# The second product of two MLPs by seven block products instead of eight

## The chip, the cores and the metric

The kernel runs on one core of a Trainium2 chip (trn2). The metric is the device time of one execution in microseconds. A profiled execution also leaves a trace of every instruction. Engines are named as in the profile: PE is the matrix engine (PEld its weight loads), DVE the vector engine, ACT the scalar engine, POOL the GpSimd engine, SP the engine that issues most DMAs.

## The reference

One sequence of 512 tokens of width 1024 goes through two layers. Layer 0 mixes tokens with a state-space scan, layer 1 with stick-breaking attention; each mixer is followed by an MLP of width 4096. Every sub-layer is residual and ends in a layer norm. All data are float32.

```python
def squared_relu_mlp(h, w1, w2):
    return jnp.square(jax.nn.relu(h @ w1)) @ w2

def reference(x, ...):
    h = x                                    # (1, 512, 1024)
    for layer in range(2):                   # w1[layer]: (1024, 4096), w2[layer]: (4096, 1024)
        mix = mamba2_mixer(h, ...) if layer == 0 else stick_breaking_attention(h, ...)
        h = layer_norm(ALPHA * h + mix, ln_mix_g[layer], ln_mix_b[layer])
        h = layer_norm(ALPHA * h + squared_relu_mlp(h, w1[layer], w2[layer]),
                       ln_mlp_g[layer], ln_mlp_b[layer])
    return h
```

## The kernel before

**Number format.** Every float32 matrix is split into two parts, `hi` (the value rounded to the matrix engine's format, made by a copy) and `lo` (the value less `hi`, made by a subtraction). A product `a @ b` is then three matmuls into the same bank of PSUM: hi·hi, hi·lo and lo·hi (`mm3`, lines 162 to 164). One matmul has a stationary block of 128 x 128 and moves 512 columns, or 256 in some stages.

**The stream of weights.** All weights are cut into tiles of 128 x 1024 float32 (512 KB) and put into one list, `stream`, in the order of their use. `emit_w` handles one tile: the DMA from memory into a buffer `raw` (line 139, issued by SP), the copy to `hi` on ACT (line 145), and the subtraction that gives `lo` on DVE (line 147; in the first stage of the kernel some are on POOL). `load_w` hands out the next tile and has those after it emitted. During an MLP there are four buffers for `raw` and six pairs for `hi` and `lo` (four in the pool `wp`, two in the pool of the MLP), used in turn.

**The MLP** (`mlp`). The 4096 inner units are made in two halves of 16 blocks of 128 units. For each block, 24 matmuls (8 blocks of the depth by three) with the weights stationary and the 512 tokens moving give one bank `f1`. ACT takes it through ReLU and square (lines 356 and 357) into `r`, DVE makes the pair `hid` from it (lines 364 and 365). The first four blocks of a layer are made in `mlp_first`, by halves of the tokens. After 16 blocks `tok_out` forms the second product of this half: for each half `n` of the 1024 output columns, four banks for the four blocks of 128 tokens (`t`), with the activations stationary and 512 columns of weights moving; one weight tile holds two blocks of the depth and serves 24 matmuls. Each bank is added into the residual `v` by DVE (line 253 in the first half, which also scales by ALPHA; line 255 in the second).

**The end of an MLP.** In the second half and second column half, the last four weight tiles are taken group by group of tokens: by pairs of token blocks in layer 0 (`PAIRS`), by single blocks in layer 1. So a group is finished while the matmuls of the next group still run. For a finished group DVE takes statistics (line 257), `Norm.__call__` aggregates them (line 289), POOL makes the reciprocal root (lines 291 and 292), DVE shifts and scales the row (lines 295 and 299), and for layer 1 SP writes it out. In layer 0 `Norm.turn` transposes the row blocks on PE (line 330) and makes their pair on ACT and DVE (lines 333 and 334); the attention's first projections `pv`, `pq` and `pk` of the first 256 tokens can begin when the first pair of token blocks is turned.

**Order.** The program is written in one order; a planner in the compiler of the kernel language fixes from it, before the run, the order of instructions of each engine's queue, filling an engine's idle time with later work whose inputs and buffers it expects to be ready. Each engine then runs its queue in that fixed order and waits on semaphores.

Of the kernel before, what the change touches and what calls it, by code (L numbers as in the profile page):

```python
# [29 lines left out]
ALPHA = (2 * 2) ** 0.25  # L30
# [5 lines left out]
def trunk(ctx: ExitStack, tc: tile.TileContext, io):  # L36
    nc = tc.nc
# [3 lines left out]
    wp = ctx.enter_context(tc.tile_pool(name="wp", bufs=4))  # L41
# [42 lines left out]
    stream = []  # L84
    marks = []
    for g in range(G):
# [7 lines left out]
        if g % 4 == 3:  # L94
            stream += [io["w_so"][g // 4, n, i] for n in range(2) for i in range(4)]

    def mlp_stream(layer):
        for half in range(2):
            for m in range(16):
                stream.append(io["w1"][layer, half * 16 + m])  # L100
            for n in range(2):
                for i in range(8):
                    stream.append(io["w2"][layer, half, n, i])

    marks.append(len(stream))
    mlp_stream(0)
# [8 lines left out]
    stream += [io["w_o"][0, i] for i in range(4)] + [io["w1"][1, 0]]  # L115
    stream += [io["w_o"][1, i] for i in range(4)] + [io["w1"][1, 1]]
    marks.append(len(stream))
    mlp_stream(1)
    del stream[marks[2]:marks[2] + 2]
# [2 lines left out]
    taken = [0]  # L122
    extra = [None, 0, 0, True, 0]
    alt = {}

    def emit_w():
# [8 lines left out]
        if pool is not None and i % (2 + rb) >= 2:  # L135
            raw = pool.tile([P, 1024], F32, tag="rawx", name=f"wr{i}", bufs=rb)
# [8 lines left out]
        nc.scalar.copy(hi, raw)  # L145
        eng = nc.gpsimd if extra[3] and i % 4 == 1 else nc.vector
        eng.tensor_sub(lo, raw, f(hi))  # L147
# [12 lines left out]

    def mm3(out, a, b, start, stop, skip=False):
        nc.tensor.matmul(out, a[0], b[0], start=start, stop=False, skip_group_check=skip)  # L162
        nc.tensor.matmul(out, a[0], b[1], start=False, stop=False, skip_group_check=skip)  # L163
        return nc.tensor.matmul(out, a[1], b[0], start=False, stop=stop, skip_group_check=skip)  # L164

    def proj(out, w, r, c0=0, c1=T):
        for _ in proj_steps(out, w, r, c0, c1):
            pass
# [8 lines left out]
    class Filler:  # L177
# [4 lines left out]
        def add(self, gen):  # L182
            self.queue.append(gen)
# [152 lines left out]
    PAIRS = [(0, 1), (2, 3)]  # L336

    M0 = 4

    def mlp_first(layer, ln, ws):  # L340
        ws = ws + [load_w(io["w1"][layer, m]) for m in range(len(ws), M0)]
        pts = [psum("mm", [P, T], f"f1_{layer}0{m}") for m in range(M0)]
        for c in range(2):
            for m in range(M0):
                proj(pts[m], ws[m], ln.hl, c * 256, c * 256 + 256)
        return pts

    def mlp(layer, ln, nxt, pts):
        v, (hh, hl) = ln.v, ln.hl
        with tc.tile_pool(name=f"mlp{layer}", bufs=2, reuse_waits="tile") as mp:  # L350
            for half in range(2):
                hid = []

                def evac(m, pt):
                    r = mp.tile([P, T], F32, tag="r", name=f"r{layer}{half}{m}", bufs=2)
                    nc.scalar.activation(r, pt, AF.Relu)  # L356
                    nc.scalar.activation(r, r, AF.Square)  # L357
                    if m == 0:
                        hid.append(tuple(mp.tile([P, KD, T], F32R, tag="hid" + s, name=f"hd{layer}{half}0{s}", bufs=1)
                                         for s in "hl"))  # L360
                    elif m == 8:
                        hid.append(act_pair(f"hd{layer}{half}1"))
                    a, b = hid[m // 8]
                    nc.vector.tensor_copy(a[:, m % 8, :], r)
                    nc.vector.tensor_sub(b[:, m % 8, :], r, f(a[:, m % 8, :]))

                m0 = 0
                if half == 0:
                    m0 = M0
                    for m in range(M0):  # L370
                        evac(m, pts[m])
                    extra[:] = [mp, 2, 2, False, marks[1 + 2 * layer]]
                for m in range(m0, 16):
                    w = load_w(io["w1"][layer, half * 16 + m])
                    pt = psum("mm", [P, T], f"f1_{layer}{half}{m}")
                    proj(pt, w, (hh, hl))
                    evac(m, pt)

                def act(k, t):
                    a = hid[k // 8]  # L380
                    return tuple(x[:, k % 8, t * P:(t + 1) * P] for x in a)

                if half == 1:
                    nxt.load_rows(lambda j, c0: mp.tile([P, T if nxt.final else D], F32,
                                                        tag=f"lnr{j}{c0 if nxt.final else 0}",
                                                        name=f"lnr{layer}{j}{c0}", bufs=1),
                                  T if nxt.final else D)
                tok_out(f"f2_{layer}{half}", act, io["w2"][layer, half], v, half == 0, ("bg", "mm"),
                        None if half == 0 else ([(t,) for t in range(NT)] if nxt.final else PAIRS),
                        None if half == 0 else nxt)  # L390
        extra[:] = [None, 0, 0, False, 0]

    def ssm(sp, nxt_ln):
        x_h, x_l = act_pair("x_")
# [380 lines left out]
    def attention(ln, nxt):  # L775
        v, h_ = ln.v, ln.hl
# [3 lines left out]
        with tc.tile_pool(name="att", bufs=2, reuse_waits="tile") as at:  # L780
# [72 lines left out]
            def ao(*args):  # L853
                for _ in ao_steps(*args):
                    pass
# [17 lines left out]
            def ao_late(tt, turn):  # L873
                p0, p1 = ([psum(("mm", "bg")[n], [P, T], f"al{n}{t}") for t in tt] for n in range(2))
                if turn is None:
                    units_end = pin[0]
                    ao(p0, 0, tt, (6,), 6, 7)
                    w_1.append(load_w(io["w1"][1, 0]))
                    pin[0] = units_end
                with tc.issue_after(pin[0]):  # L880
                    if turn is None:
                        ao(p1, 1, tt, range(7), 0, 7)
                        ao(p0, 0, tt, (7,), 6, 7)
                    else:
                        ao(p0, 0, tt, (6, 7), 6, 7)
                    ao_evac(p0, 0, tt)
                    if turn is not None:
                        ao(p1, 1, tt, range(7), 0, 7)
                        w_1.append(load_w(io["w1"][1, 1]))
# [103 lines left out]
            w_o, wv_of, w_1, pin = {}, {}, [], [None]  # L993
# [4 lines left out]
            pts = [psum("mm", [P, T], f"p{'qk'[j]}0") for j in range(2)]  # L998
# [41 lines left out]
            pts = mlp_first(1, nxt, w_1)  # L1040
# [67 lines left out]
```

## Time and profile before

| | |
|---|---|
| median of 3 runs | 1461.16 us (1459.86 to 1462.78) |
| profiled execution, device time | 1463.09 us |
| its span, first to last instruction | 1460.7 us |
| PE busy | 1435.9 us (98%) |
| DVE busy | 864.2 us (59%) |
| ACT busy | 661.8 us (45%) |
| POOL busy | 219.9 us (15%) |
| mean granted PE clock | 0.996 |
| DMA | 129.43 MB, mean 89 GB/s |

Busy time is the union of an engine's instructions; matmuls overlap each other in the records, so a busy PE says only that no gap is seen. In a line of the groups, the figures after the bar are the busy time, the mean duration of one instruction in ns, and the engine's idle time just before them with what ended it. In a timeline, the columns are the start, the duration, and in brackets the idle time before the instruction and what released it. A table by windows gives the busy time of each engine in each stretch, the instructions in brackets, then the granted PE clock, the share of the DMA engines and GB/s.

### The profile page before, as it was taken

The page shows a single profiled execution, that of the slowest core. Times are in us where ns is not written, and L with a number is a line of the kernel's source. Part 1 is how long each engine was busy: PE and PEld are TensorE (multiplying, and loading weights), DVE is VectorE, ACT ScalarE, POOL GpSimd, SP SyncE. Part 2 cuts the span into 40 slices and gives each one's busy share as a digit, 9 for nine tenths or more (in the row PEclk, how much of TensorE's full clock was granted, in tenths as well). Part 3 has the DMA queues.
Part 4 walks back from the last instruction along what each step waited for, and adds up shares of the span by engine and source line. Part 5 has one row for each costly group of instructions (what it writes and reads, how often), then busy time and mean ns, then how long its engine had stood idle before and what let it go on. Part 6 is the DMA issues. An engine that isn't in the chain of part 4 may idle for free. (4 is left out here: it accounts for less than half of the span.)

```text
span 1460.7 us, 19159 instructions
## 1 busy us (share of the span) xinstructions
PE 1435.9 (98%) x7606; PEld 1235.5 (85%) x7606; DVE 864.2 (59%) x1274; ACT 661.8 (45%) x1072; POOL 219.9 (15%) x243
## 2 busy tenths in 40 slices
PE   8999999999999999999999999999999999999997
PEld 6898897888987988888888988898879888888886
DVE  5799897568877643234323667787866432244334
ACT  5566663346652442124322178888824332134210
POOL 2345554134442100000000100000000000000001
PEclk9999999999999999999999999999999999999999
DMA  5233222222123422332331121121224423322311
GB/s 180 73 101 103 71 73 73 87 87 71 60 73 127 161 91 98 101 94 94 101 100 61 57 87 58 44 73 59 73 64 137 132 87 101 102 92 95 101 44 58
DMA packets 37481, 129.43 MB, mean 89 GB/s; under 512 B 4496, under 2 KB 4752, under 8 KB 37392
## 3 DMA queue, kind: packets, MB, share of 16 engines
q1 hardware_dynamic: 34800, 123.88, 26.2%
q10 hardware_dynamic: 2592, 4.33, 1.0%
q8 instruction: 60, 0.98, 0.3%
q14 instruction: 29, 0.24, 0.1%
HBM read 126.10 MB, written 2.10 MB: 88 GB/s over the span
## 5 line engine op out<-in xcount | busy, mean ns | idle before, releaser
L147 DVE TENSOR_TENSOR wl<-wr,wh 128x1024 fp32r<-128x1024 f32 x202 | 249.3, 1235 | 432.0 <-ACT wh L145 431.4
L145 ACT CAST wh<-wr 128x1024 fp32r<-128x1024 f32 x219 | 230.3, 1053 | 542.9 <-PE f L164 252.6
L163 PE MATMUL f<-ln_hl,wh 128*128 128x512 f32 (+1 forms) x544 | 201.2, 371 | 0.0
L164 PE MATMUL f<-ln_hh,wl 128*128 128x512 f32 (+1 forms) x544 | 201.1, 370 | 0.0
L162 PE MATMUL f<-ln_hh,wh 128*128 128x512 f32 (+1 forms) x544 | 200.4, 371 | 0.0
L291 POOL TENSOR_SCALAR ln_rs<-ln_mv 128x2 f32<-128x2 f32 (+1 forms) x10 | 8.2, 816 | 739.5 <-DVE ln_mv L289 739.5
L164 PEld LDWEIGHTS f<-ln_hh,wl 128*128 128x128 f32 x544 | 102.3, 188 | 17.5
L163 PEld LDWEIGHTS f<-ln_hl,wh 128*128 128x128 f32 x544 | 102.3, 188 | 17.5
L162 PEld LDWEIGHTS f<-ln_hh,wh 128*128 128x128 f32 x544 | 101.9, 188 | 17.5
L164 PE MATMUL pz<-wh,x_l 128*128 128x256 f32 x256 | 72.7, 284 | 0.0
L163 PE MATMUL pz<-wl,x_h 128*128 128x256 f32 x256 | 72.5, 283 | 0.0
L162 PE MATMUL pz<-wh,x_h 128*128 128x256 f32 x256 | 72.3, 283 | 0.0
L147 POOL TENSOR_TENSOR wl<-wr,wh 128x1024 fp32r<-128x1024 f32 x17 | 43.6, 2562 | 93.4 <-ACT wh L145 93.0
L162 PE MATMUL px<-x_h,wh 128*128 128x512 f32 x128 | 50.8, 397 | 0.0
L163 PE MATMUL px<-x_l,wh 128*128 128x512 f32 x128 | 50.3, 393 | 0.0
L164 PE MATMUL px<-x_h,wl 128*128 128x512 f32 x128 | 50.2, 393 | 0.0
L163 PEld LDWEIGHTS pz<-wl,x_h 128*128 128x128 f32 x256 | 48.7, 190 | 0.9
L162 PEld LDWEIGHTS pz<-wh,x_h 128*128 128x128 f32 x256 | 48.7, 190 | 0.8
L164 PEld LDWEIGHTS pz<-wh,x_l 128*128 128x128 f32 x256 | 48.7, 190 | 0.4
L357 ACT ACTIVATE r<-r 128x512 f32<-128x512 f32 x64 | 40.4, 633 | 1.9
L356 ACT ACTIVATE r<-f 128x512 f32<-128x512 f32 x64 | 37.9, 591 | 6.0 <-PE f L164 5.9
L920 POOL TENSOR_TENSOR u<-u 128x128 f32<-128x128 f32 x16 | 7.8, 487 | 211.9 <-DVE u L918 211.9
(1369 smaller groups left out, 3842.0 us busy)
## 6 DMA issues: line engine op xcount, KB each, us to landing
wr<-w SPq DMA_DIRECT2D x128, 512.0 KB, 3.5
wr<-w_bc SPq DMA_DIRECT2D x16, 512.0 KB, 3.5
wr<-w_x SPq DMA_DIRECT2D x16, 512.0 KB, 3.5
wr<-w_z SPq DMA_DIRECT2D x16, 512.0 KB, 3.5
wr<-w_so SPq DMA_DIRECT2D x16, 512.0 KB, 3.5
wr<-w_qk SPq DMA_DIRECT2D x16, 512.0 KB, 3.5
wr<-w_v SPq DMA_DIRECT2D x8, 512.0 KB, 3.5
wr<-w_o SPq DMA_DIRECT2D x8, 512.0 KB, 3.4
```

The lines of the kernel that those rows point to most:

```text
L145: nc.scalar.copy(hi, raw)
L147: eng.tensor_sub(lo, raw, f(hi))
L162: nc.tensor.matmul(out, a[0], b[0], start=start, stop=False, skip_group_check=skip)
L163: nc.tensor.matmul(out, a[0], b[1], start=False, stop=False, skip_group_check=skip)
L164: return nc.tensor.matmul(out, a[1], b[0], start=False, stop=stop, skip_group_check=skip)
L291: nc.gpsimd.tensor_scalar(rs, self.mv[:, t0:t1, 1], LN_EPS, None, ALU.add)
L356: nc.scalar.activation(r, pt, AF.Relu)
L357: nc.scalar.activation(r, r, AF.Square)
L920: nc.gpsimd.tensor_add(e4[:, n:], e[:, P:2 * P], e[:, 2 * P:])
```

## The change

The inner units of each MLP are made in four quarters of 8 blocks of 128. In each quarter the second product is a matrix product of 512 tokens x 1024 units by 1024 units x 1024 columns, and it is cut into 2 x 2 blocks in tokens, units and columns and formed by seven block products (P1 to P7, Winograd's variant of Strassen's scheme) instead of eight. One block product uses two weight tiles; for each of them it has 12 matmuls (two token blocks by two depth blocks by three), so 24 in all. The matmuls have the same shape as before.

What is added or moved:

- The activations' four sums and the splits of seven operands (`prepare`, called twice in a quarter, after the fourth and the eighth block of units). The quarter's inner units stay in a tile `R`. Copies for `hi` are on ACT, sums and `lo` on DVE, each on 128 x 512 elements. The old copy to `hid` and its subtraction are gone.
- The weights' sums t1 to t4. They need the tiles of `w2` eight times per pass `s` instead of four (fetched again rather than kept), four extra subtractions of 128 x 1024 on DVE per pass, and seven split tiles instead of four. Two passes make a quarter.
- The buffers: two for `raw` instead of four, two each for t1 (`rawa`) and t2 (`rawc`); the six `hi`/`lo` pairs remain. `load_w` emits four tiles ahead instead of two in the MLP.
- The adds into `v`: 16 of 128 x 512 in a quarter. Bank pair X takes P1, is added to `v`, then P6 is accumulated onto it, it is added again, then P7, and it is added to two blocks of `v`. Bank pair Y takes P5, is added, then P3 is accumulated onto it and it is added.
- The end of an MLP: the last quarter's statistics and norm for the token blocks 0 and 1 follow P7, those for 2 and 3 follow P3 (by single blocks in layer 1). In layer 0 the turn of the blocks 0 and 1 is written between the two weight tiles of P3. The rows of the norm's gain and bias go to a tile of the pool `act`.
- The blocks of a quarter are made in the order 0, 4, 1, 5, 2, 6, 3, 7.

```diff
+    M_ORDER = (0, 4, 1, 5, 2, 6, 3, 7)
+    def w2_items(layer, q):
+        ...
+        for s in range(2):
+            key = (layer, q, s)
+            for nm, item in (("P1", b(0, 0, s)),
+                             ("P5", ("t1", key, b(0, 1, s), b(0, 0, s))),
+                             ("P6", ("t2", key, b(1, 1, s))),
+                             ("P4", ("t4", key, b(1, 0, s))),
+                             ("P7", ("t3", key, b(0, 0, s))),
+                             ("P2", b(1, 0, s)),
+                             ("P3", b(1, 1, s))):
...
     def mlp_stream(layer):
-        for half in range(2): ...
+        for q in range(4):
+            for m in range(8):
+                stream.append(w1_tile(layer, 8 * q + m))
+            for items in w2_items(layer, q).values():
+                stream.extend(items)
...
     def emit_w():
+        item = stream[i]
+        if not isinstance(item, tuple):
+            raw = fetch(item)
+        elif item[0] == "t1":
+            raw = sums[item[1]] = fetch(item[2], "rawa")
+            nc.vector.tensor_sub(raw, raw, fetch(item[3]))
+        elif item[0] == "t2":
+            raw = fetch(item[2], "rawc")
+            nc.vector.tensor_sub(raw, raw, sums[item[1]])
+            sums[item[1]] = raw
         else:
-            raw = wp.tile([P, 1024], F32, tag="raw", name=f"wr{i}", bufs=2)
-        nc.sync.dma_start(raw, stream[i])
+            raw = fetch(item[2])
+            if item[0] == "t3":
+                nc.vector.tensor_sub(raw, sums[item[1]], raw)
+            else:
+                nc.vector.tensor_sub(raw, raw, sums[item[1]])
...
-        prefetch(1 + 2)
+        prefetch(1 + depth[0])
...
+            extra[:] = [mp, 2, 0, False, marks[1 + 2 * layer]]
+            depth[0] = 4
+            def add(row, n, pts, stats=False, js=(0, 1)):
+                for j in js:
+                    t = rows[row][j]
+                    vs = v[:, t, n * T:(n + 1) * T]
+                    if (t, n) in started:
+                        nc.vector.tensor_add(vs, pts[j], vs)
+                    else: ...
+                    if stats:
+                        nc.vector.bn_stats(nxt.st[:, t, n, :], vs)
...
+                def prepare(c):
+                    ...
+                    def split(nm, src):
+                        h, l = (x[:, ks, :] for x in A[nm])
+                        nc.scalar.copy(h, src)
+                        nc.vector.tensor_sub(l, src, f(h))
+                    split("P1", a11)
+                    nc.vector.tensor_add(s1, a21, a22)
+                    nc.vector.tensor_sub(s2, s1, a11)
+                    nc.vector.tensor_sub(a21, a11, a21)
+                    split("P5", s1)
+                    split("P6", s2)
+                    split("P4", a22)
+                    split("P7", a21)
+                    split("P2", a12)
+                    nc.vector.tensor_sub(a12, a12, s2)
+                    split("P3", a12)
...
+                X = bank("bg", "X")
+                product("P1", X)
+                add(1, 0, X)
+                Y = bank("bg", "Y")
+                product("P5", Y)
+                add(2, 1, Y)
+                product("P6", X, False)
+                add(1, 1, X)
+                ...
+                Z = bank("mm", "Z")
+                product("P4", Z)
+                add(2, 0, Z)
+                product("P7", X, False)
+                add(2, 0, X, last)
+                add(2, 1, X, last)
+                if last:
+                    for g in ([(0,), (1,)] if nxt.final else [(0, 1)]):
+                        nxt(g)
+                Z = bank("mm", "V")
+                product("P2", Z)
+                add(1, 0, Z, last)
+                if not last:
+                    product("P3", Y, False)
+                    add(1, 1, Y)
+                elif nxt.final:
+                    ws = None
+                    for j in range(2):
+                        ws = product("P3", Y, False, (j,), None, ws)
+                        add(1, 1, Y, True, (j,))
+                        nxt((rows[1][j],))
+                else:
+                    product("P3", Y, False, mid=lambda: nxt.turn(rows[2]))
+                    add(1, 1, Y, True)
+                    nxt(rows[1])
+                    nxt.turn(rows[1])
```

More of the change, by code (lines that the diff above doesn't have):

```diff
@@ L95, in trunk, with w1_tile, b @@
             stream += [io["w_so"][g // 4, n, i] for n in range(2) for i in range(4)]
-    def mlp_stream(layer):
[L98 to L103, printed above, removed]
+    M_ORDER = (0, 4, 1, 5, 2, 6, 3, 7)
+    def w1_tile(layer, i):
+        return io["w1"][layer, 8 * (i // 8) + M_ORDER[i % 8]]
+    def w2_items(layer, q):
+        def b(row, n, s):
+            return io["w2"][layer, q // 2, n, 4 * (q % 2) + 2 * row + s]
+        r = {}
+        for s in range(2):
[7 more added lines that the diff above has]
+                             ("P3", b(1, 1, s))):
+                r.setdefault(nm, []).append(item)
+        return r
+    def mlp_stream(layer):
+        for q in range(4):
[3 more added lines that the diff above has]
+                stream.extend(items)
     marks.append(len(stream))
@@ L114, in trunk @@
     alt_o = len(stream) + 3
-    stream += [io["w_o"][0, i] for i in range(4)] + [io["w1"][1, 0]]
-    stream += [io["w_o"][1, i] for i in range(4)] + [io["w1"][1, 1]]
+    stream += [io["w_o"][0, i] for i in range(4)] + [w1_tile(1, 0)]
+    stream += [io["w_o"][1, i] for i in range(4)] + [w1_tile(1, 1)]
     marks.append(len(stream))
@@ L124, in trunk @@
     alt = {}
+    sums = {}
+    depth = [2]
     def emit_w():
@@ L340, in mlp_first @@
     def mlp_first(layer, ln, ws):
-        ws = ws + [load_w(io["w1"][layer, m]) for m in range(len(ws), M0)]
+        ws = ws + [load_w(w1_tile(layer, m)) for m in range(len(ws), M0)]
         pts = [psum("mm", [P, T], f"f1_{layer}0{m}") for m in range(M0)]
@@ L348, in mlp, with part @@
     def mlp(layer, ln, nxt, pts):
[L349 to L352, printed above, removed]
+        v, h_ = ln.v, ln.hl
+        W = P * 2
+        rows = {1: (2, 3), 2: (0, 1)}
+        cols = {1: slice(W, 2 * W), 2: slice(0, W)}
+        started = set()
+        with tc.tile_pool(name=f"mlp{layer}", bufs=1, reuse_waits="tile") as mp:
+            extra[:] = [mp, 2, 0, False, marks[1 + 2 * layer]]
[6 more added lines that the diff above has]
+                        nc.vector.tensor_add(vs, pts[j], vs)
+                    else:
+                        started.add((t, n))
+                        nc.vector.scalar_tensor_tensor(vs, vs, ALPHA, pts[j], ALU.mult, ALU.add)
+                    if stats:
+                        nc.vector.bn_stats(nxt.st[:, t, n, :], vs)
+            for q in range(4):
+                last = q == 3
+                R = act_tile(f"r{layer}{q}")
+                L = act_tile(f"l{layer}{q}", F32R).rearrange("p (a k) (b t) -> p a (k b) t", a=4, b=2)
+                def part(nm):
+                    return mp.tile([P, 4, W], F32R, tag=nm, name=f"{nm}{layer}{q}")
+                A = {nm: (part("h" + nm), L[:, i] if i < 4 else part("l" + nm))
+                     for i, nm in enumerate(("P1", "P5", "P6", "P7", "P2", "P3", "P4"))}
@@ L354, in evac @@
                 def evac(m, pt):
-                    r = mp.tile([P, T], F32, tag="r", name=f"r{layer}{half}{m}", bufs=2)
+                    r = R[:, m, :]
                     nc.scalar.activation(r, pt, AF.Relu)
                     nc.scalar.activation(r, r, AF.Square)
[L358 to L387, printed above, removed]
@@ L388, in mlp @@
-                tok_out(f"f2_{layer}{half}", act, io["w2"][layer, half], v, half == 0, ("bg", "mm"),
-                        None if half == 0 else ([(t,) for t in range(NT)] if nxt.final else PAIRS),
-                        None if half == 0 else nxt)
+                def prepare(c):
+                    ks, k2 = slice(2 * c, 2 * c + 2), slice(4 + 2 * c, 6 + 2 * c)
+                    a11, a21, a12, a22 = R[:, ks, cols[1]], R[:, ks, cols[2]], R[:, k2, cols[1]], R[:, k2, cols[2]]
+                    s1, s2 = (mp.tile([P, 2, W], F32, tag=nm, name=f"{nm}{layer}{q}{c}") for nm in ("u1", "u2"))
+                    def split(nm, src):
[13 more added lines that the diff above has]
+                    split("P3", a12)
@@ new lines, in mlp, with bank @@
+                for i in range(8):
+                    if q == 0 and i < M0:
+                        pt = pts[i]
+                    else:
+                        w = load_w(w1_tile(layer, 8 * q + i))
+                        pt = psum("mm", [P, T], f"f1_{layer}{q}{i}")
+                        proj(pt, w, h_)
+                    evac(M_ORDER[i], pt)
+                    if i % 4 == 3:
+                        prepare(i // 4)
+                items = w2_items(layer, q)
+                def bank(tag, nm):
+                    return [psum(tag, [P, T], f"{nm}{layer}{q}{j}") for j in range(2)]
@@ new lines, in product @@
+                def product(nm, pts, start=True, js=(0, 1), mid=None, ws=None):
+                    ah, al = A[nm]
+                    ws = {} if ws is None else ws
+                    for s in range(2):
+                        if s not in ws:
+                            ws[s] = load_w(items[nm][s])
+                        if s == 1 and mid is not None:
+                            mid()
+                        for kk in range(2):
+                            k, c = 2 * s + kk, slice(kk * T, (kk + 1) * T)
+                            for j in js:
+                                x = slice(j * P, (j + 1) * P)
+                                mm3(pts[j], (ah[:, k, x], al[:, k, x]), (ws[s][0][:, c], ws[s][1][:, c]),
+                                    start and k == 0, k == 3, skip=True)
+                    return ws
@@ new lines, in mlp @@
+                X = bank("bg", "X")
[7 more added lines that the diff above has]
+                if last:
+                    lnr = act_tile(f"lnr{layer}").rearrange("p k t -> p (k t)")
+                    wd = T if nxt.final else D
+                    nxt.load_rows(lambda j, c0: lnr[:, j * D + c0:j * D + c0 + wd], wd)
@@ L391, in mlp @@
         extra[:] = [None, 0, 0, False, 0]
+        depth[0] = 2
     def ssm(sp, nxt_ln):
@@ L877, in ao_late @@
                     ao(p0, 0, tt, (6,), 6, 7)
-                    w_1.append(load_w(io["w1"][1, 0]))
+                    w_1.append(load_w(w1_tile(1, 0)))
                     pin[0] = units_end
@@ L888, in ao_late @@
                         ao(p1, 1, tt, range(7), 0, 7)
[L889 removed]
+                        w_1.append(load_w(w1_tile(1, 1)))
                         nxt.turn(turn)
```

12 lines of the change are left out of this document (10 added, 2 removed).

## The prediction

> **What bounds the kernel now.** I read the page first, then the MLPs by windows, then single tiles, then timelines of the places where an MLP ends.
>
> ```profile
> span 1460.7 us, 19159 instructions
> PE 1435.9 (98%) x7606; PEld 1235.5 (85%) x7606; DVE 864.2 (59%) x1274; ACT 661.8 (45%) x1072; POOL 219.9 (15%) x243
> PEclk9999999999999999999999999999999999999999
> L147 DVE TENSOR_TENSOR wl<-wr,wh 128x1024 fp32r<-128x1024 f32 x202 | 249.3, 1235 | 432.0 <-ACT wh L145 431.4
> L145 ACT CAST wh<-wr 128x1024 fp32r<-128x1024 f32 x219 | 230.3, 1053 | 542.9 <-PE f L164 252.6
> ```
>
> A busy PE alone proves little, so the stretches of the two MLPs: second product (566 to 655), blocks of units (655 to 740), the end of layer 0 (800 to 830), the last second product and what follows it.
>
> ```profile
> core 0: us, PE busy (x) PEld busy (x) DVE busy (x) ACT busy (x) POOL busy (x), PEclk, DMA share, GB/s
> 566.00:655.00 89.00, 89.00 (x394) 73.68 (x394) 25.82 (x25) 19.00 (x19) 0.00 (x0) 1.00 0.29 95
> 655.00:740.00 85.00, 85.00 (x377) 70.38 (x376) 35.37 (x48) 32.75 (x46) 0.00 (x0) 1.00 0.31 99
> 800.00:830.00 30.00, 30.00 (x169) 26.19 (x168) 18.87 (x25) 5.06 (x7) 3.08 (x3) 1.00 0.13 38
> 1369.00:1452.00 83.00, 83.00 (x367) 68.41 (x365) 30.29 (x39) 10.55 (x10) 5.14 (x6) 1.00 0.17 56
> 1452.00:1461.00 9.00, 0.03 (x1) 0.00 (x0) 4.42 (x7) 0.00 (x0) 1.71 (x2) 0.67 0.30 110
> ```
>
> PE has no gap and the full clock until 1452, while DVE works 26 of 89 us in a second product. ACT and DVE wait for PE (the two groups above), not PE for them. So PE's pace sets the MLPs, and 9 us of norm and output stand behind its last matmul. The pace, from the inner units' tile (its users, first and last start):
>
> ```profile
> L356 ACT ACTIVATE r<-f x64: 577/592/601, 489.9 to 1365.8; 128x512 f32<-128x512 f32 x64
> L357 ACT ACTIVATE r<-r x64: 622/634/636, 490.5 to 1366.4; 128x512 f32<-128x512 f32 x64
> L364 DVE CAST hd001h<-r x8: 427/428/428, 524.5 to 562.6; 128x512 fp32r<-128x512 f32 x8
> L365 DVE TENSOR_TENSOR hd001l<-r,hd001h x8: 692/694/694, 525.0 to 563.1; 128x512 fp32r<-128x512 f32 x8
> L364 DVE CAST hd010h<-r x8: 427/428/428, 655.1 to 693.2; 128x512 fp32r<-128x512 f32 x8
> ```
>
> From block 8 of one half (524.5) to block 0 of the next (655.1) lie 8 x 24 + 384 = 576 matmuls in 130.6 us: 0.2267 us each; 562.6 - 524.5 over 7 x 24 gives the same. The Trainium skill ("TensorE: Matmul & The Clock Gate", the section that begins "Wait") has N / 2.4 GHz plus 2.5 ns, 0.2157 us at 512 columns; by that the first term below would be 41.4 us. The trace is slower, and its row decides.
>
> **The change, part by part.**
>
> *PE.* Before, 2 layers x 2 halves x 2 column halves x 16 depth blocks x 4 token blocks x 3 = 1536 matmuls in second products; after, 8 quarters x 7 products x 24 = 1344. 192 fewer x 0.2267 = **-43.5 us**, if PE stays fed. A product now takes 5.44 us, a weight tile 2.72 us instead of 5.44, a quarter 192 + 168 = 360 matmuls, 81.6 us.
>
> *DVE, total.* The slots, start to start:
>
> ```profile
> 501.61 1.23 DVE L147 TENSOR_TENSOR wl<-wr,wh 128x1024 fp32r<-128x1024 f32 x1 [1.01 <-ACT wh L145]
> 502.77 0.43 DVE L364 CAST hd000h<-r 128x512 fp32r<-128x512 f32 x1
> ...
> 1452.06 0.69 DVE L255 TENSOR_TENSOR v<-f,v 128x512 f32<-128x512 f32 x1 [0.45 <-PE f L164]
> 1452.79 0.69 DVE L257 BATCH_NORM_STATS2 ln_st<-v 128x6 f32<-128x512 f32 x1
> 1453.52 0.21 DVE L289 BATCH_NORM_AGGREGATE ln_mv<-ln_st 128x2 f32<-128x12 f32 x1
> 1453.76 1.42 DVE L295 SCALAR_TENSOR_TENSOR v<-v,ln_mv,lnr 128x512 f32<-128x512 f32 x2
> 1455.64 1.41 DVE L299 SCALAR_TENSOR_TENSOR v<-v,ln_rs,lnr 128x512 f32<-128x512 f32 x2 [0.46 <-POOL ln_rs L292]
> ```
>
> A 128x1024 subtraction holds DVE 1.16 us, a 128x512 one 0.73. Per quarter: 22 `lo` and 8 weight sums x 1.16 = 34.8; `prepare` 22 x 0.73 = 16.1; 16 adds x 0.73 = 11.7; together 62.6 of 81.6 us. ACT: 22 copies x 1.05, 8 blocks x 1.23, 14 split copies at about 0.63 (row L357, same size) = 41.8 us. On average PE stays the bound. But within the seven products (38.1 us) DVE has `prepare` of the second four blocks 8, sums and `lo` of nine to ten tiles 17, `lo` of four next `w1` tiles 5, fourteen adds 10: 40 us. So the cover is gone there, and order decides.
>
> *Weight supply.* Splitting runs ahead as far as buffers allow:
>
> ```profile
> 0.00:655.00 655.00, 105.95 (x85) 45.97 (x18) 1.00 0.30 96
> wr<-w SPq DMA_DIRECT2D x128, 512.0 KB, 3.5
> q1 hardware_dynamic: 34800, 123.88, 26.2%
> ```
>
> At 655 (row of line 147 alone: DVE 85, POOL 18) 103 tiles are split and PE uses the 98th: five ahead, the six pairs less one. So P1 to the first half of P6 begin with tiles in stock. Thereafter one of two `raw` buffers must per tile take the DMA 3.5, for t3 and t4 a sum 1.16, the copy 1.05 and `lo` 1.16: 7 us with a sum, 5.8 without, against 5.44 of demand per pair. The DMA engines themselves have room: 26.2% of 1460.7 us over 123.88 MB is 1.6 us for a tile, 16 tiles 26 of 38.1 us.
>
> I laid DVE's queue out by hand from the start of P1 (0 us), earlier program first. The last block is out of ACT at 1.5; `prepare` holds DVE to about 8; `lo` of P6's second tile; P1's adds 10.0 to 11.5 (P6 overwrites their bank from 10.9, the second block from 11.6); P4's `lo` at 12.7 and 13.8 (needed 16.3 and 19.0); P7's at 19.8 and 20.9 (21.8, 24.5); the second adds of X 20.9 to 22.4 (P7 wants the banks at 21.8 and 22.4); P2's at 25.7 and 26.9 (27.2, 29.9); P3's at 31.5 and 32.6 (32.6, 35.4); the next `w1` at 37.3 (38.1). Nothing stalls, but the lead is 1 to 2 us everywhere. A DMA half a microsecond later in each of four rounds uses it up. Bounds: 0 if the layout holds; 3 us a quarter if every round also waits for one pair of adds (4 x 1.46, less the lead). I take 0.75 a quarter, nearer the layout: **+6** (0 to 24).
>
> *The end of layer 1.* Before, DVE's last row cost 5 us behind PE (the timeline above), since every earlier row was done under 5.44 us of matmuls. After, blocks 0 and 1 get their last values from P7, 10.9 us before PE's end, and all norms lie behind that on DVE: 4 adds and 4 statistics 5.84; two rows x (0.24 + 1.46 + 1.45) = 6.3; P2's 2 adds and statistics 2.9; P3's two blocks x (1.46 + 3.15) = 9.2; one wait for POOL 0.46: 24.7 us. From DVE's end to the end of the span stays what it is, 1460.7 - 1457.05 = 3.65. So the span ends at -10.9 + 24.7 + 3.65 = 17.5 us after PE instead of 8.7: +8.8 without backlog; P3's two `lo` (2.3) fall into the same time. **+11** (9 to 14).
>
> *The end of layer 0.* Before, the first projections cover the last norm exactly:
>
> ```profile
> 815.78 2.48 DVE L299 SCALAR_TENSOR_TENSOR v<-v,ln_rs,lnr 128x1024 f32<-128x1024 f32 x2 [0.90 <-POOL ln_rs L292]
> 823.93 0.68 DVE L255 TENSOR_TENSOR v<-f,v 128x512 f32<-128x512 f32 x1
> 831.08 2.49 DVE L299 SCALAR_TENSOR_TENSOR v<-v,ln_rs,lnr 128x1024 f32<-128x1024 f32 x2 [0.91 <-POOL ln_rs L292]
> 823.28 0.28 PE L162 MATMUL pv<-wh,ln_hh 128*128 128x256 f32 x1
> 835.22 1.48 PE L330 MATMUL ln_b<-ident,v 128*128 128x128 f32 x12
> ```
>
> Blocks 0 and 1 were scaled 5 us before the last matmul of the MLP, and the projections of their 256 tokens filled PE from 823.28 to 835.22 while DVE did the other pair. After, the chain from P7 is: adds and statistics 5.84, P3's `lo` 2.3, shift and scale of two blocks with POOL 6: 14 us, 3 behind PE's end; then P2's adds 2.9 and four `lo` of the turn (0.73 each) interleave, so projections start some 5 us late after the transposes; and the other pair, behind `lo` of the attention's first tiles, another 2 or so beyond their 12 us. **+7** (3 to 12).
>
> *Costed at nothing.* The split copies and 24 more weight copies a layer on ACT (above, half busy). The order of blocks. The `lnr` rows on ACT's queue, issued after P6, 3.3 us before use at most against 10 at hand. Writes to `out` on SP: no weights are behind them. Fetching t1's two tiles lies in stock time.
>
> *Sum.* -43.5 + 6 + 11 + 7 = -19.5. The profiled execution took 1463.09 around its span of 1460.7, 2.4 outside, and is 1.9 above the median. Against the median: 1461.16 - 19.5 = **1441.7 us**.
>
> **The rivals.**
>
> 1. *Everything hides* (0.10). Steady quarters without a stall, layer 0's end with 1 us: -43.5 + 9 + 1 = -33.5, 1427.7. For it: the hand layout; DVE has slack in the block stage, 24 of 43.5 us. Against it: 40 us of DVE in 38.1, and at layer 1's end no order avoids 24.7 us.
>
> 2. *The second product becomes DVE's* (slower, 0.13). Each queue is run in its fixed order, and an add that waits for PE, or a sum that waits for its DMA, holds back the `lo` behind it; the two `raw` buffers then hand the delay to the next DMA. Break-even is (43.5 - 11 - 7) / 8 = 3.2 us a quarter. With one pair of adds (1.46) in each of four rounds and the ordinary waits of half a slot (0.6) at seven DVE steps, less 2 of lead: about 8 us, of which the next block stage, where a tile is wanted only every 5.44 us, is taken to win back 3. 8 x 5 = 40: -43.5 + 40 + 18 = +14.5, 1475.7. For it: two buffers instead of four, and rounds of 7 us against 5.44. Against it: five tiles of stock and 34 us of work that is truly due before the next `w1`. The Trainium skill ("TensorE: Matmul & The Clock Gate", "Architectural detail") calls the queues of ACT and DVE strict first-in first-out, which is what this rival needs. In the trace such a wait is the 0.45 us before the add at 1452.06, which held up nothing.
>
> 3. *Stalls eat most of it* (0.20). 2 us a quarter with both ends near their upper bounds: -43.5 + 16 + 13 + 10 = -4.5, 1456.7; within 0.2% (2.9 us, about what a measurement here can tell from no change) it ends if a quarter costs 2.5. Half a microsecond in each place decides between this and my forecast.
>
> **How the numbers follow.** The forecast, -8 to -33, has 0.57; rival 1 0.10, rival 2 0.13, rival 3 0.20, of which 0.06 is within 0.2%. Faster 0.57 + 0.10 + 0.14 = 0.81, same 0.06, slower 0.13. The range leaves out rival 2 and the far ends: from 1427 (rival 1; the lower bounds sum to -31.5) to 1459 (rival 3 with 2.3 a quarter).
>
> **What would show it.** Matmuls 7414; second products with 168 in about 38 us a quarter; PE's waits by `wh`/`wl` (weight supply), by `v` adds on X (bank reuse) or by the split tiles. At layer 1's end, DVE without a gap from P7 on, and 17 to 20 us behind the last matmul instead of 8.7. At layer 0's end, a PE gap of some 5 us before the first `pv`. DVE at about 77% of the span (864 us, plus 8 x 62.6 for the quarters, less some 248 for what both MLPs give it now). The forecast is wrong if a quarter's seven products take over 41 us (rival 2 or 3), or if the pace of a matmul changes when its stationary block comes from `prepare`'s tiles, which no row of before can show.

## The result and the profile after

| | before | after |
|---|---|---|
| median of four runs | 1461.39 us (1459.86 to 1462.78) | 1435.41 us (1434.33 to 1436.57) |
| profiled execution: time, span | 1463.09, 1460.7 us | 1435.05, 1433.1 us |

The ratio is 0.9823, 95% interval 0.9806 to 0.9840: 26 us faster; 1441.7 was forecast, 1427 to 1459. The page of the changed kernel, its engines and the two groups that were shown of before:

```profile
span 1433.1 us, 19282 instructions
PE 1396.4 (97%) x7414; PEld 1202.4 (84%) x7414; DVE 1085.5 (76%) x1530; ACT 772.0 (54%) x1232; POOL 219.1 (15%) x243
PEclk9999999999999999999999899999999999999998
L190 ACT CAST wh<-wr 128x1024 fp32r<-128x1024 f32 x235 | 246.7, 1050 | 343.1 <-DMA wr<-w 173.3
L192 DVE TENSOR_TENSOR wl<-wr,wh 128x1024 fp32r<-128x1024 f32 x218 | 268.3, 1232 | 181.7 <-ACT wh L190 180.8
```

192 matmuls are gone, DVE has 221 us more to do, and ACT now waits more for DMA than for PE. Yet the list of whom PE waited for (us in total, times, the longest), over the whole execution, has only one new line:

```profile
PE ln_b L375 <- DVE v L344: 6.4, 2, 4.5
```

Both waits lie at the end of layer 0. In the products PE waited for nothing that the profile shows: neither for weights (`wh`, `wl`) nor for banks nor for operands. By PE's starts the 168 matmuls of each of the first three quarters of a layer take 38.08 us (516.62 to 554.70 for the first), 0.2267 us each. To see where the time went I cut both traces at four instructions of PE: the first transpose and the last transpose (first and last start in the row of `ln_b`), and the last matmul of each MLP.

Before:

```profile
L330 PE MATMUL ln_b<-ident,v x96: 270/272/277, 467.2 to 1113.6; 128*128 128x128 f32 x96
823.05 0.39 PE L164 MATMUL f<-wh,hd011l 128*128 128x512 f32 x1
1451.64 0.39 PE L164 MATMUL f<-wh,hd111l 128*128 128x512 f32 x1
```

After:

```profile
L375 PE MATMUL ln_b<-ident,v x96: 270/273/476, 467.0 to 1101.0; 128*128 128x128 f32 x96
799.27 0.39 PE L209 MATMUL Y<-wh,lP 128*128 128x512 f32 x1
1417.35 0.39 PE L209 MATMUL Y<-wh,lP 128*128 128x512 f32 x1
```

| stretch | before | after | difference |
|---|---|---|---|
| first transpose to last matmul of layer 0's MLP | 355.9 | 332.3 | -23.6 |
| from there to the last transpose (attention) | 290.5 | 301.7 | +11.2 |
| to the last matmul of layer 1's MLP | 338.0 | 316.3 | -21.7 |
| to the end of the span | 9.1 | 15.8 | +6.7 |

96 matmuls x 0.2267 us are 21.8. Layer 0 gives 1.9 more only because 16 transposes that stood among its matmuls now stand behind them; so its end costs 11.2 - 1.9 = 9.3. The account: -43.5 for the matmuls, +9.3, +6.7.

The 9.3 is not exact, since the granted clock differs elsewhere in the attention too. In the trace of before it was 0.64 from 864 to 866 us and 0.51 from 866 to 868, which cost some 1.5 us; the trace of a kernel further down (all quarters by eight products) has 1.00 there. In the trace of after it was at 0.50 for some 7 us around 1058, in that of before for some 3.5 us at the same place, which cost some 1.1 us more. Without both, the end of layer 0 would cost 9.7, an estimate from these stretches.

The end of layer 0 in PE's timeline:

```profile
804.21 1.11 PE L375 MATMUL ln_b<-ident,v 128*128 128x128 f32 x4 [4.54 <-DVE v L344]
807.13 2.82 PE L375 MATMUL ln_b<-ident,v 128*128 128x128 f32 x12 [1.82 <-DVE v L344]
809.61 0.56 PE L207 MATMUL pv<-wh,ln_hh 128*128 128x256 f32 x1
...
810.61 0.41 PE L209 MATMUL pv<-wh,ln_hl 128*128 128x256 f32 x1
810.82 0.41 PE L207 MATMUL pv<-wh,ln_hh 128*128 128x256 f32 x1
```

The same place by windows (the granted clock is the third number from the right):

```profile
799.00:809.00 10.00, 3.64 (x16) 2.75 (x16) 10.00 (x12) 2.96 (x4) 5.00 (x9) 0.66 0.58 197
809.00:814.00 5.00, 5.00 (x31) 5.00 (x30) 5.00 (x9) 1.47 (x3) 0.94 (x2) 0.65 0.35 109
```

PE stands, then does transposes and projections of 256 columns 0.21 us apart where they were 0.12 apart before. The 0.66 and 0.65 are means: by finer windows the clock is 0.50 from 803 to 812 us and 1.00 again from 813. DVE is busy for all 10.00 of the first 10 us.

Within the products DVE is nearly full too. Two quarters of layer 0 by windows, which begin and end some 2 us before the products do (these lie from 516.62 to 554.70 and from 679.82 to 717.90 us):

```profile
514.00:552.40 38.40, 38.40 (x171) 31.81 (x170) 33.52 (x41) 15.83 (x20) 0.00 (x0) 1.00 0.54 166
678.00:716.00 38.00, 38.00 (x169) 31.48 (x168) 28.89 (x37) 14.78 (x18) 0.00 (x0) 1.00 0.45 144
```

Some neighbours in DVE's timeline:

```profile
523.04 1.22 DVE L192 TENSOR_TENSOR wl<-wr,wh 128x1024 fp32r<-128x1024 f32 x1
524.17 0.68 DVE L443 TENSOR_TENSOR u<-u,r 128x512 f32<-128x512 f32 x1
524.77 0.68 DVE L444 TENSOR_TENSOR r<-r 128x512 f32<-128x512 f32 x1
525.38 0.68 DVE L439 TENSOR_TENSOR l<-u,hP 128x512 fp32r<-128x512 f32 x1
525.98 0.68 DVE L411 SCALAR_TENSOR_TENSOR v<-v,X 128x512 f32<-128x512 f32 x1
526.58 1.22 DVE L192 TENSOR_TENSOR wl<-wr,wh 128x1024 fp32r<-128x1024 f32 x1
```

That is 33.5 and 28.9 us of DVE in these windows; between the exact times of the products it is 32.1 and 28.6, where I had put 40. And from start to start a 128x512 instruction holds DVE for 0.60 us here, not the 0.73 that I read from a chain in which each one needs the one before. The same trace has such a pair too: the sum of line 443 at 498.15 us reads that of line 442 at 497.43 and starts 0.72 us after it, and the next one, which needs neither, 0.61 us later.

### The profile page after: what moved, and what is told of

Read it like the earlier page. It is cut to its first block, busy times and chain, and to the rows that moved or that the text cites. A ratio compares the mean times of both kernels' runs of the same rounds, so it can differ in the third digit from the quotient of the medians.

```text
span 1433.1 us, 19282 instructions
## 1 busy us (share of the span) xinstructions
PE 1396.4 (97%) x7414; PEld 1202.4 (84%) x7414; DVE 1085.5 (76%) x1530; ACT 772.0 (54%) x1232; POOL 219.1 (15%) x243
## 5 line engine op out<-in xcount | busy, mean ns | idle before, releaser
L190 ACT CAST wh<-wr 128x1024 fp32r<-128x1024 f32 x235 | 246.7, 1050 | 343.1 <-DMA wr<-w 173.3
L192 DVE TENSOR_TENSOR wl<-wr,wh 128x1024 fp32r<-128x1024 f32 x218 | 268.3, 1232 | 181.7 <-ACT wh L190 180.8
L208 PE MATMUL X<-wl,hP 128*128 128x512 f32 x192 | 74.7, 389 | 0.0
L207 PE MATMUL X<-wh,hP 128*128 128x512 f32 x192 | 74.5, 389 | 0.0
L209 PE MATMUL X<-wh,l 128*128 128x512 f32 x192 | 74.0, 389 | 0.0
L438 ACT CAST hP<-r 128x512 fp32r<-128x512 f32 x80 | 48.1, 620 | 31.6 <-DVE r L450 30.7
L208 PE MATMUL Y<-wl,hP 128*128 128x512 f32 x128 | 49.8, 389 | 0.0
```

The costliest lines, as they stand in the source:

```text
L438: nc.scalar.copy(h, src)
```

## The experiments

All edits are to the changed kernel, and differences are against its median of 1435.41 us. It was not run again beside them; the kernel before was, with medians of 1461.30 to 1462.48 us, so a difference of about 1 us says little.

### Eight products in the last quarter of both layers

```diff
+    CLASSIC = (0, 1)
...
+                if last and layer in CLASSIC:
+                    ...
+                    tok_out(f"f2_{layer}", act, Half(), v, False, ("bg", "mm"),
+                            [(t,) for t in range(NT)] if nxt.final else PAIRS, nxt)
+                    continue
                 items = w2_items(layer, q)
```

with the stream and `prepare` to match (four splits instead of seven, no sums). `Half` hands `tok_out` the weight tiles of the quarter, `act` its split activations. The next kernel has `CLASSIC = (0,)`.

> The last quarter of each layer is done with eight block products (96 x 2 matmuls, the end by groups of token blocks as in the kernel before); the other six quarters keep seven. Theory A (the two ends cost the changed kernel about 6.7 and 9.3 us because eight adds, the statistics and all norms come after P7): both costs go, PE gets 2 x 24 x 0.2267 = 10.9 us more: -16.0 + 10.9 = -5, 1430. Theory B (the ends cost that for other reasons, such as the place of the norm rows or two prefetched tiles more): +11, 1446.

Measured: 1428.36 us (1427.45 to 1430.06), ratio to before 0.9769 (0.9756 to 0.9783): 7 us faster than the changed kernel, with 48 matmuls more. It has no wait at the end of layer 0, and the windows there are full again:

```profile
800.00:830.00 30.00, 30.00 (x233) 28.88 (x233) 19.13 (x26) 9.57 (x16) 5.15 (x9) 1.00 0.16 54
```

Theory A holds. Its median is the lowest of the study; the range of the next kernel overlaps its own.

### Eight products in the last quarter of layer 0 alone

> The last quarter by eight block products in layer 0 alone. Theory A (each end has its own price, 9.3 us in layer 0 and 6.7 to 7.3 us in layer 1, against 5.4 us of matmuls): layer 0 gives 4 of the 7 us that the last quarter of both layers gave, 1431 to 1432. Theory B (nearly all of it came from the end of layer 1, where the last row's norm stands bare): 1434 to 1435.

Measured: 1429.27 us (1428.12 to 1430.61), 6.1 us faster than the changed kernel. So by the medians most of the 7 us is layer 0's, the opposite of theory B, and layer 1's edit gives 0.9, within the spread. The traces divide it more plainly. From the first transpose to the last (the MLP of layer 0, its end and the attention) the changed kernel takes 634.0 us, this one 628.4 and the one with eight products in both layers 630.1; from there to the end of the span they take 332.1, 332.1 and 330.2. So layer 0's edit gives 3.9 to 5.6 us, near A's 4, and layer 1's 1.9: there 5.4 us of matmuls buy back 7.3 us of norm. The two traces with the same layer 0 differ by 1.7 us mainly because the clock was 0.50 from 849 to 851 us in one of them and 1.00 in the other.

### All quarters by eight products

> All eight quarters by eight block products, with the quarters, their buffers, fetches of each tile once, and the ends by groups. Theory A (PE's matmuls are all that the seven products save in a steady quarter): six quarters x 24 x 0.2267 = 32.6 us more than the kernel with eight products in the last quarter of each layer alone: 1461, the time of the kernel before, though DVE has 16 us a quarter less to do. Theory B (part of the gain comes from quarters instead of halves, or seven products cost hidden stalls of 1 us a quarter): 1450 to 1456.

Measured: 1460.76 us (1459.42 to 1462.14), ratio to before 0.9992 (0.9983 to 1.0001). Against eight products in the last quarters alone it is 32.4 us for 6 x 24 = 144 matmuls, 0.225 us each. Theory A: quarters, buffers and order give nothing by themselves, and the seven products of a steady quarter hide everything that they add.

### A dose of DVE work

```diff
                         nc.vector.scalar_tensor_tensor(vs, vs, ALPHA, pts[j], ALU.mult, ALU.add)
+                    for _ in range(1 if cur[0] < 3 else 0):
+                        nc.vector.tensor_sub(dose, zero, zero)
...
                 last = q == 3
+                cur[0] = q
```

The second kernel has a 2 in place of the 1.

> One extra subtraction of 128 x 512 on DVE beside every add of a product in the first three quarters of each layer, 16 a quarter, on operands of its own: 16 x 0.60 to 0.73 = 10 to 12 us of DVE a quarter, six quarters. Theory A (queue order and slots of about 0.60 for independent instructions leave DVE 5 us or more of room within the products, and work that is not yet due can slide into the next block stage): under 2 us a quarter, 1436 to 1447. Theory B (the prediction's hand layout, a lead of 1 to 2 us): 8 to 10 us of stall in each of six quarters, less a third regained: 1470 to 1490.

> Two extra subtractions of 128 x 512 on DVE beside every add in the first three quarters of each layer, 32 a quarter, some 19.5 us of DVE. The first dose of 16 (9.8 us) cost 15 us over six quarters, some 2.3 us each. Theory A (DVE has a room of 7 us within the products, and beyond it each us of DVE becomes a us of PE): 2.3 + 9.8 = 12 us a quarter, 1505 to 1512. Theory B (work that is not due slides into the block stage, where DVE is half idle, so about a quarter of a dose shows at any size): 4.6 us a quarter, 1462 to 1466.

Measured, one execution each: 1450.38 and 1462.77 us, 15 and 27.4 more than the changed kernel. The first had lost 2.2 us before its first MLP (first transpose at 469.2 instead of 467.0), where it had nothing new to do; so 2.1 and 4.6 us a quarter, for 9.6 and 19.2 us of DVE at 0.60. The first lies a little above theory A; the second is theory B of its row. PE's waits in layer 0 of the second kernel, beside that at the layer's end:

```profile
PE Z L208 <- DVE wl L192: 4.2, 2, 2.8
PE X L207 <- DVE v L415: 1.9, 1, 1.9
PE X L209 <- DVE l L446: 0.6, 1, 0.6
PE Y L208 <- DVE wl L192: 0.5, 1, 0.5
```

On average about a quarter of an added microsecond comes through, but not evenly. By PE's starts the products of the six quarters with a dose took 8.5, 4.7, 0, 4.3, 3.6 and 5.1 us longer than 38.08 in the second kernel, and 6.8, 0, 0, 4.3, 0.5 and 1.7 in the first. Nor is all of it waiting. After four of the waits in the second kernel (those of 2.83, 1.85, 2.45 and 1.92 us) the granted clock went to 0.50 for some 3 us, from 529 to 532 us for one, and the matmuls started 0.43 us apart instead of 0.23; that makes some 6 of its 27.4 us. The waits are those that the prediction named (weights for the fourth product, X's bank, an operand's `lo`), with a far smaller size.

### Four pairs of split weights

```diff
-            extra[:] = [mp, 2, 0, False, marks[1 + 2 * layer]]
+            extra[:] = [mp, 0, 0, False, marks[1 + 2 * layer]]
```

> The MLP's two extra hi and lo pairs are left out: four pairs, so three tiles in stock ahead of PE's instead of five; no work added. Theory A (the stock of five is what covers the burst of sums and the DMA rounds within the products): 1 to 4 us of waits for weights in each of eight quarters, 1443 to 1467. Theory B (DMA, copies and subtractions keep up tile by tile, and the stock is not drawn on): within 2 us of the changed kernel, 1433 to 1437.

Measured, one execution: 1449.74 us, 14.3 more. PE's waits in layer 0:

```profile
PE V L207 <- ACT wh L190: 2.6, 3, 1.3
PE Y L207 <- ACT wh L190: 1.9, 4, 0.8
```

They stand at P2 and P3, the end of a quarter (V and Y are their banks), where the copies have fallen behind. By PE's marks layer 0's MLP took 6.7 us more than in the changed kernel and layer 1's 8.5. The two lines sum to 4.5 of the 6.7. Part of the rest is that a wait is counted from the end of the matmul before it, 0.39 us after its start, where the next one otherwise starts after 0.23; what else is in it stays open. So the stock is drawn on and needed: 1.8 us a quarter with two tiles fewer in it, none with five. Theory A.

### Matmuls without use in layer 0's gap

```diff
+                    hot = psum("mm", [P, 4, P], f"hot{layer}")
+                    for _ in range(20):
+                        nc.tensor.matmul(hot, ones_r, ones_r.unsqueeze(1).to_broadcast([P, 4, P]), start=True, stop=True)
                     add(1, 1, Y, True)
                     nxt(rows[1])
                     nxt.turn(rows[1])
```

> Twenty matmuls without use (ones by ones, 128 x 512, into a bank of their own) stand behind P3 of layer 0, in the gap of 4.7 us before the first transposes. Theory A (the gap itself is DVE's, but the granted clock of 0.65 from 809 to 814 us is because PE was idle, and costs about 2.8 us in transposes and the first projections): clock near 1.00 there, 2 to 3 us faster, 1432.5 to 1433.5. Theory B (those matmuls are slow because their operands come in late): no gain, or the twenty matmuls push the transposes back by up to 1 us: 1435 to 1436.5.

Measured: 1432.40 us (1431.27 to 1434.96), ratio to before 0.9801 (0.9787 to 0.9816). The intervals of the two ratios overlap, but PE's timeline shows that the clock is kept, as theory A has it:

```profile
799.06 4.29 PE L521 MATMUL hot<-ones_r 128*128 128x512 f32 x18
803.19 0.83 PE L375 MATMUL ln_b<-ident,v 128*128 128x128 f32 x4
806.02 1.53 PE L375 MATMUL ln_b<-ident,v 128*128 128x128 f32 x12 [2.00 <-DVE v L344]
807.30 0.37 PE L207 MATMUL pv<-wh,ln_hh 128*128 128x256 f32 x1
```

By windows:

```profile
809.00:814.00 5.00, 4.99 (x41) 4.99 (x42) 5.00 (x7) 0.00 (x0) 1.86 (x2) 1.00 0.24 92
```

Twelve transposes take 1.53 us instead of 2.82, and the clock is 1.00 in the window that had 0.65. From the last matmul of the MLP to the last transposes of the second pair it is 19.2 us (798.83 to 818.06) instead of 21.1 (799.27 to 820.39), 1.9 less. Of this 0.6 lies before the first transposes, which the clock does not explain; so some 1.3 of the 9.3 us are shown to be the clock's. The rest of the 3.0 us between the medians is not: in the traces 1.1 us of it is the longer stretch at 0.50 around 1058 in the changed kernel, far behind the filler. The Trainium skill ("TensorE: Matmul & The Clock Gate", "Part 1: The HAM clock gate") says that PE falls to half its rate after an idle window of about 3.4 us and regains it after as long a busy one. The half rate agrees with the 0.50 in the changed kernel. The times agree roughly: the clock fell at about 802.3 us, 2.6 us after the last matmul's end (799.66), and came back at about 812.5, 5.4 us after PE began to work without a gap (807.13); both times are estimates from the means of the windows around them.

### Late subtractions on POOL

```diff
-        eng = nc.gpsimd if extra[3] and i % 4 == 1 else nc.vector
+        late = marks[1] <= i < marks[1] + 4 or i >= marks[3] - 2
+        eng = nc.gpsimd if late or extra[3] and i % 4 == 1 else nc.vector
```

> The lo subtractions of the attention's first four tiles and of layer 1's last two tiles go from DVE to the idle POOL; all else as changed. Theory A (after P7 DVE's queue is what is late at both ends): DVE loses 4 x 1.16 us between P7 and the projections of layer 0 and up to 2.3 us between P7 and the last norm of layer 1, so the end of layer 0 shortens by 2 to 4.5 us, the end of layer 1 by 1 to 2 us: 3 to 6 us faster than the changed kernel, 1429 to 1432. Theory B (the ends are late by their chain of dependent steps, from PE through adds, statistics, POOL's root, shift and scale, and what stands between on DVE is filler in its waits): no change, 1434 to 1437. If POOL's reads slow DVE down: slower.

Measured: 1439.72 us (1438.29 to 1442.04), 4.3 slower: a miss for theory A, and the last sentence of the expectation came true. The first wait at layer 0's end grew from 4.5 to 10.1 us. DVE's timeline there, a shift beside POOL's work and one without:

```profile
795.60 3.46 DVE L341 SCALAR_TENSOR_TENSOR v<-v,ln_mv,lnr 128x1024 f32<-128x1024 f32 x1
801.44 1.27 DVE L341 SCALAR_TENSOR_TENSOR v<-v,ln_mv,lnr 128x1024 f32<-128x1024 f32 x1
```

POOL's timeline:

```profile
795.58 2.38 POOL L193 TENSOR_TENSOR wl<-wr,wh 128x1024 fp32r<-128x1024 f32 x1 [301.17 <-ACT wh L190]
...
801.45 0.22 POOL L337 TENSOR_SCALAR ln_rs<-ln_mv 128x2 f32<-128x2 f32 x1
...
804.13 2.34 POOL L193 TENSOR_TENSOR wl<-wr,wh 128x1024 fp32r<-128x1024 f32 x1
...
807.13 1.01 POOL L338 TENSOR_TENSOR ln_rs<-ln_rs,mhalf 128x2 f32<-128x2 f32 x1
```

Two things went wrong. A shift on DVE that ran beside POOL's subtraction took 3.46 us instead of 1.27. And the reciprocal root of the first pair's norm (line 338) stood in POOL's queue behind other work, among it a 2.34 us subtraction, from 801.7 to 807.1. In DVE's queue the scale of the first pair now came behind the second pair's statistics and shifts, at 808.68 us instead of 802.87; the scale of the second pair waited for its root:

```profile
808.68 2.50 DVE L345 SCALAR_TENSOR_TENSOR v<-v,ln_rs,lnr 128x1024 f32<-128x1024 f32 x2
814.10 2.48 DVE L345 SCALAR_TENSOR_TENSOR v<-v,ln_rs,lnr 128x1024 f32<-128x1024 f32 x2 [2.92 <-POOL ln_rs L338]
```

How much each of the two cost was not separated. At the end of layer 1 the edit did shorten the time behind the last matmul, from 15.8 to 14.3 us (1437.9 less 1423.64).

### The same in layer 1 alone, with eight products at layer 0's end

> Eight block products in the last quarter of layer 0, seven in that of layer 1, whose last two weight tiles get their lo on POOL. Theory A (at the end of layer 1 DVE alone is late, POOL's roots come later than those two subtractions): the 1.5 us that the same edit took off behind the last matmul in the earlier run: 1427.5 to 1428.2, level with eight products in both layers. Theory B (POOL's reads slow DVE's shifts as they did at the end of layer 0): 1429 to 1431.

Measured: 1429.90 us (1428.32 to 1430.67) against 1429.27 without: no gain that shows. From the last matmul to the end it is 14.9 instead of 15.8 us (1428.1 less 1413.21; 1427.5 less 1411.73), so 0.9 of the hoped 1.5, and this execution's attention ended 1.5 us later, before the edit acts (the clock was 0.50 from 849 to 851 us, where the other's was 1.00). Whether the edit saves time stays open.

## Why the prediction was right, and where its terms were off

**PE's term** held: -43.5 forecast, -21.7 found in each layer, and 0.225 us a matmul from the kernel with eight products throughout. The pace with operands from `prepare` is the same, 38.08 us for 168 matmuls. The Trainium skill's spacing ("TensorE: Matmul & The Clock Gate", the section that begins "Wait") would have given 41.4, an estimate from that page's figure; the runs bear out the trace's 0.2267 us.

**The quarters' stalls**, +6 (0 to 24): 0. The step "within the seven products DVE has 40 us in 38.1" was mis-sized: 28.6 to 32.1 us in the six steady quarters. The slot of 0.73 came from the norm's dependent chain; independent instructions follow each other after 0.60, which for the 25 of `prepare` and the adds takes 3 us off. Most of the other 5 are weights: the first quarter's products hold 15 of the quarter's 30 sums and `lo` of 128x1024, some 17 us, where I had put 22. So the lead was not the 1 to 2 us that I named: the doses show that even 9.6 us more of DVE cost 2.1 on average, and nothing in two of six quarters.

**The end of layer 1**, +11 (9 to 14): +6.7, below its lower end. The mechanism is as told: DVE goes on without a gap from P7's adds. The same 0.73 was the largest error. Its last stretch:

```profile
1408.26 2.48 DVE L408 TENSOR_TENSOR v<-X,v 128x512 f32<-128x512 f32 x4
1410.65 1.87 DVE L413 BATCH_NORM_STATS2 ln_st<-v 128x6 f32<-128x512 f32 x3
1412.44 1.21 DVE L192 TENSOR_TENSOR wl<-wr,wh 128x1024 fp32r<-128x1024 f32 x1
...
1424.62 2.72 DVE L340 SCALAR_TENSOR_TENSOR v<-v,ln_mv,lnr 128x512 f32<-128x512 f32 x4
1427.26 2.73 DVE L344 SCALAR_TENSOR_TENSOR v<-v,ln_rs,lnr 128x512 f32<-128x512 f32 x4
```

From 1408.26 to 1429.99 are 21.7 us with one `lo`, 20.6 without, against 24.7 reckoned: sixteen adds and statistics at 0.60 instead of 0.73 (2.1), shifts and scales at 1.33 a row instead of 1.46 (1.0), aggregates (0.5), and no wait for POOL (0.46). Besides, the adds began 1.3 us after P7's last matmuls, behind a `lo`, and from DVE's end to the end of the span it was 3.1 us instead of 3.65. Counted as in the prediction, 15.4 us lie behind PE's end, where I had named 17 to 20 as a sign.

**The end of layer 0**, +7 (3 to 12): +9.3. The gap "of some 5 us" was 4.54 + 1.82. What I left out is the clock after it, 0.50 until 812 us: 1.3 to 1.9 us by the filler matmuls.

**The rivals.** The first had the quarters right (no stall at all), but not the ends. The second, DVE as the bound of the products, needed 3.2 us a quarter; two extra instructions beside each add came to 4.6, so it lay some 14 us of DVE work a quarter away, by a line between the two doses. The third fell with it.

**The sum.** The mechanism and the large term held. That the total came within 6.3 us of the forecast is in part luck: the quarters and layer 1 were forecast too dear by 6 and 4.3 us, layer 0's end too cheap by 2.3.

Against the median the difference is 26.0, by the spans of the two profiled executions 27.6: that of before was 1.9 above its median, as the prediction said.

## What to carry to other kernels

Where one engine's matmuls set the pace, an algorithm with fewer of them pays in full in the steady stages as long as its extra sums fit on idle engines with a few tiles of stock ahead. It loses at the seams, where one stage ends and the next begins. Look for the place where the last results of several rows all come late, and use the plain scheme there: here 24 matmuls more at one seam gave back more than they cost. Read a slot's length from neighbours like those that the change will have: dependent ones gave 0.73 us, independent ones 0.60. An idle engine is not free help when another engine's chain runs through its queue.

## What the runs showed that I had not expected

- Around a gap of 4.54 us PE's clock went to 0.50, from 803 to 812 us; matmuls without use in the gap kept it at 1.00, and the stretch was 1.9 us shorter. A stretch at 0.50 also stood in the attention of some traces and not of others and cost some 1.5 us there, so a difference of that size between two traces needs a look at the clock.
- A DVE instruction with two inputs in SBUF took 3.46 us instead of 1.27 while POOL did a subtraction of 128x1024.
- Only some 23% of the work added to a DVE that was already busy for 28.6 to 32.1 of 38.08 us came through to the time, from nothing in one quarter to 8.5 us in another, part of it by the clock.
